# Attention outputs divided once per pair of heads, paired score banks, keys stacked by transfers, and TensorE held to program order

## The chip, the core and the metric

The kernel runs on one core of a Trainium2 chip. A core has TensorE (PE; its weight loads are shown as PEld), VectorE (DVE), ScalarE (ACT), GpSimd (POOL) and SyncE (SP, which here only issues transfers), and DMA queues that move data between its memories. Each engine works through its own instructions in their order and waits on semaphores for the others. The metric is the device time of one execution in microseconds (us).

## The reference

One layer of a diffusion backbone over 128 context tokens and 512 latent tokens with 1024 features. Two attention mixers are read in parallel from one input projection, merged, and followed by an MLP. What matters here, shortened:

```python
def _block_attention(q, k, v):                # mixer A: 8 query heads, 2 key heads
    s = einsum('bqgrd,bkgd->bgrqk', qblk, k) * scale
    p = softmax(s, axis=-1)
    return einsum('bgrqk,bkgd->bqgrd', p, v)

def _neighbourhood_attention(...):            # mixer B: 8 heads, a window of keys and a bias
    s_loc = where(col_mask, s_loc + bias, NEG_INF)
    p = softmax(concatenate([s_loc, s_ctx]), axis=-1)
    return p[..., :n_loc] @ v_window + p[..., n_loc:] @ ctx_v

a_o = _block_attention(aq, concat([ctx_ak, ak]), concat([ctx_av, av]))
b_o = _neighbourhood_attention(bq, bk, bv, ctx_bk, ctx_bv, nat_bias)
m = sigmoid(ga) * (a_o @ w_br_a) + sigmoid(gb) * (b_o @ w_br_b)
x = x + gate1 * (m @ w_out)
x = x + gate2 * (square(relu(h2 @ w_mlp_in)) @ w_mlp_out)
```

Latent queries of A read 128 context keys and 512 latent keys (640 columns); those of B read windows of 384 or 512 columns. Context queries read only context keys.

## The kernel before

Features lie on the 128 partitions, tokens (640 = 128 + 512) along the columns; a half is 320 columns. Each number is carried as a rounded upper part (`h`) and a rest (`l`), both float32r, and a product is three matmuls: upper x upper, upper x lower, lower x upper (`gemm_k`, L339 to L341). Each weight tile of 128 output features arrives by a transfer (`wst`), ACT makes its upper part (L301), POOL or DVE its lower part (L302). One tile of the input projection is 2 halves x 8 blocks x 3 = 48 matmuls of 320 columns.

**Stages.** A first stage makes norms and three tiles: A's keys, the first two query heads, A's values. Then comes attention (from about 59.5 us to 345 us), then the merge with the remaining gates, the output projection and the MLP.

**Attention.** `attention` walks through units: two heads (`HeadA`) and the context queries of that pair (`CtxPair`), four times, then the same for mixer B (`HeadB`). The score products `S` of a unit run beside the transposes `T` and value products (`pv`) of the unit before, step by step. For each block of 128 queries `S` multiplies into one or two PSUM banks (`pss`), DVE finds the maximum, ACT writes the exponentials (`pa`, `pb`) with their row sums, and `normalise` (L616) divides the weights on DVE: the row-sum's reciprocal (L618) and a product (L619). `T` transposes four blocks into a bank (`pt`, L653, L710), ACT and DVE split the result (`ph` L606, `pl` L607), and `pv`, called one step later, multiplies both with the values into `po`; `combine` adds the two halves of `po` into the output tile `ao` or `bo`, which holds two heads.

**Fill.** The other projection tiles (`AFILL`, `BFILL`: queries, keys, values, and four gates, which are stored to memory and read back in the merge, `GATES`) are cut into groups of three matmuls, and `F.spend` puts as many into each step as the constant `STEP` leaves. Work that follows a tile, such as norms, rotation and splits, is kept in `F.posts`.

**Order.** Outside the first stage a scheduler sets the order of each engine's instructions, TensorE's included. `manual_schedule` holds an engine to the order of the program; in the merge and MLP it is used for DVE.

**Keys.** A stacked key tile holds a head's keys twice, on partitions 0 to 63 and 64 to 127, since the queries' upper and lower parts lie on these halves. For A `k_both` (L568) writes both halves with ACT and DVE, in pieces; for B `k_part` writes one half and `k_dup` (L575) copies it by a transfer.

**PSUM.** One set of eight banks for the whole kernel: g 2 (fill), s 3 (scores), t 2 (transposes), o 1 (value products).

Of the kernel before, what the change touches and what calls it, by code (L numbers as in the profile page):

```python
# [42 lines left out]
Q0P = 2  # L43
# [14 lines left out]
def trunk_layer(ctx: ExitStack, tc: tile.TileContext, xT, small_in, wmodA, wmodB, tabs, cacheK, cacheV, bias,  # L58
# [10 lines left out]
    pp = ctx.enter_context(tc.tile_pool(name="pp", bufs=1, space=bass.MemoryType.PSUM))  # L69
# [27 lines left out]

    def ps_g():
        return pp.tile([P, 512], F32, tag="g", bufs=2, name="pg")

    def ps_s():
        return pp.tile([P, 512], F32, tag="s", bufs=3, name="pss")

    def ps_t():
        return pp.tile([P, 512], F32, tag="t", bufs=2, name="pt")

    def ps_o():
        return pp.tile([P, 512], F32, tag="o", bufs=1, name="po")
# [105 lines left out]
    class Weights:  # L214
# [74 lines left out]
        def conv(self):  # L289
# [4 lines left out]
            else:  # L294
# [7 lines left out]
                (nc.gpsimd if key in WPOOLSET else DVE).tensor_sub(lo, st, r32(hi))  # L302
# [207 lines left out]
    ck, cv = (kp.tile([P, NT], F32, name=x) for x in ("ck", "cv"))  # L510
    nc.sync.dma_start(ck, cacheK)
# [15 lines left out]
    def qk_norm(raw, g, h, bank=ps_g, src=None, buf=None):  # L527
        sl = HALVES[h]
        buf = buf or rf
        sq = buf("qsq")  # L530
        src = raw[:, sl] if src is None else src
        ACT.activation(sq[:, :HT], src, AF.Square)
        pt = bank()
        PE.matmul(pt[:, :HT], blk, sq[:, :HT], start=True, stop=True)
        rs = buf("qrs")
# [26 lines left out]
    def k_part(k, e, dst, src, eng=None):  # L562

        s = src[half(e)]
        ACT.activation(k[0][half(e), dst], s, AF.Copy)
        (eng or DVE).tensor_sub(k[1][half(e), dst], s, r32(k[0][half(e), dst]))

    def k_both(k, e, dst, src):  # L568

        k_part(k, e, dst, src)  # L570
        s = src[half(e)]
        ACT.activation(k[0][half(1 - e), dst], s, AF.Copy)
        DVE.tensor_sub(k[1][half(1 - e), dst], s, r32(k[0][half(e), dst]))

    def k_dup(k, e, n, q=MISC):  # L575
        for t in k:
            q.dma_start(r32(t[half(1 - e), :n]), r32(t[half(e), :n]))
# [5 lines left out]
    def v_stack(raw, cvp, bank=ps_g):  # L583
# [32 lines left out]
    def normalise(p, sm):  # L616
        rc = small("rc", 1)
        DVE.reciprocal(rc, sm)  # L618
        DVE.tensor_scalar(p, p, rc, None, op0=OP.mult)  # L619

    class HeadA:
# [3 lines left out]
        def __init__(self, hd):  # L625
            self.j, self.e, self.g = hd // 2, hd % 2, hd // 4
            self.need = ("aq", self.j)

        def S(self, qt):
# [4 lines left out]
            ps = [ps_s(), ps_s()]  # L634
            p = u("pa")
            n2, s2, nm, sm = small("n2"), small("s2"), small("nm", 1), small("sm", 1)
            for j in range(2):
                c = slice(P + j * HT, P + (j + 1) * HT)
                PE.matmul(ps[j][:, :HT], q, kh[:, c], start=True, stop=False)
                PE.matmul(ps[j][:, :HT], q, kl[:, c], start=False, stop=True)  # L640
                DVE.tensor_reduce(n2[:, j:j + 1], ps[j][:, :HT], axis=AX.X, op=OP.max, negate=True)
            DVE.tensor_tensor(nm, n2[:, 0:1], n2[:, 1:2], op=OP.min)  # L642
            for j in range(2):
                ACT.activation(p[:, HALVES[j]], ps[j][:, :HT], AF.Exp, bias=nm, accum_out=s2[:, j:j + 1])  # L644
            DVE.tensor_add(sm, s2[:, 0:1], s2[:, 1:2])
            normalise(p, sm)
            self.p.append(p)
            return 540

        def T(self, t):  # L650
# [5 lines left out]
            def pv():  # L656
# [7 lines left out]
                return 430  # L664
            return 250, pv
# [5 lines left out]
    class HeadB:  # L671
# [13 lines left out]
        def S(self, qt):  # L685
# [9 lines left out]
            mx, nm, sm = small("mx", 1), small("nm", 1), small("sm", 1)  # L695
# [3 lines left out]
            ACT.activation(p[:, :w], ps[:, :w], AF.Exp, bias=nm, accum_out=sm)  # L699
            normalise(p[:, :w], sm)  # L700
            self.p.append(p)
            return 380

        def T(self, gi):
# [9 lines left out]
            def pv():  # L714
# [11 lines left out]
                return 400  # L726
            return 230, pv

    class CtxPair:
# [28 lines left out]
        def T(self, _):  # L758
# [5 lines left out]
            def pv():  # L764
# [7 lines left out]
                return 430  # L772
            return 110, pv

    AQ, BQS, BK, BV = {}, {}, {}, {}
    AO = [None] * 4
# [11 lines left out]
    def fill_tile(n, F):  # L788
# [7 lines left out]
        for h in range(2):  # L796
# [3 lines left out]
            for k in range(KT):  # L800
                gemm_k(ps, w, H1, h, k, k, k == 0, k == KT - 1)
                yield 400
# [7 lines left out]
            else:  # L810
                if h == 0:
                    raw = o_tile("raw")
                ACT.activation(raw[:, sl], ps, AF.Copy)
            F.flush(1)
        F.flush()
        if kind == "aq":
            def last():
                qk_norm(raw, qg, 1)
                a_q_rot(j, raw)
            F.posts = [lambda: qk_norm(raw, qg, 0), last]  # L820
        elif kind == "bq":
            BQS[j] = qs
        elif kind == "bk":
            DQ[QO].dma_start(bkT[j], raw[:, 0:P])
            ckj = ck[:, (j + 1) * P:(j + 2) * P]
            BK[j] = []

            def k_post(e):
                k = (kt_tile("bkh"), kt_tile("bkl"))
                k_part(k, e, slice(P, 2 * P), ckj)  # L830
                k_part(k, e, slice(6 * P, 7 * P), ckj)
                k_part(k, e, slice(0, P), raw[:, 0:P])
                k_part(k, e, slice(2 * P, 6 * P), raw[:, P:NT])
                k_dup(k, e, 7 * P, DQ[QD])
                BK[j].append(k)
# [549 lines left out]
```

## Time and profile before

| | us |
|---|---|
| runs: median (lowest, highest) | 1001.46 (1000.43, 1001.6) |
| the profiled execution | 1000.66 |
| its span | 998.7 |
| PE busy in the span | 951.0 (95%) |
| DVE busy | 704.9 (71%) |
| ACT busy | 516.4 (52%) |
| POOL busy | 171.7 (17%) |

The page cuts the span into 40 slices of 25 us; each digit is the busy share in tenths, and PEclk the granted clock:

```profile
PE   7987899998899999999999999999999999999996
DVE  4468877788866788787677787678833884368644
PEclk8998999999999999999999999999999999999999
```

Matmuls are pipelined: one of 320 columns is in the pipe for about 310 ns, while the next starts after 147 ns. So a busy share of PE is above the share of its peak, and short waits show better in the weight loads.

### The profile page before, as it was taken

To read this page: it belongs to the slowest core of one execution; us is meant where nothing else is said; L and a number is where in the kernel's file an instruction comes from. 1 tells how busy PE (TensorE), PEld (TensorE's weight loads), DVE (VectorE), ACT (ScalarE), POOL (GpSimd) and SP (SyncE) were. 2 spreads that over 40 slices of the span, in tenths; PEclk is the share of its full clock that TensorE was granted. 3 is DMA by queue.
4 is the path that set the end of the run, shared out by engine and by line. 5 is a ranking of instruction groups with operands and counts; after the bars stand their busy time and mean duration, and the time that the engine had idled before them with its cause. 6 is when DMAs were issued, how large, how long until landed. Compare 5 with 4: busy or idle time off the path is not lost.

```text
span 998.7 us, 16550 instructions
## 1 busy us (share of the span) xinstructions
PE 951.0 (95%) x6317; PEld 906.1 (91%) x6317; DVE 704.9 (71%) x1577; ACT 516.4 (52%) x1117; POOL 171.7 (17%) x153
## 2 busy tenths in 40 slices
PE   7987899998899999999999999999999999999996
PEld 5776778887888999999999899999999999999996
DVE  4468877788866788787677787678833884368644
ACT  4475667666655664654333563237611663156542
POOL 0342232211322010200041200012200220012100
PEclk8998999999999999999999999999999999999999
DMA  9842101222443445654742243212221233120312
GB/s 348 207 169 73 32 28 40 69 49 77 122 102 94 133 154 189 215 155 163 238 135 80 69 148 107 86 63 84 90 84 40 85 101 90 64 71 37 107 42 106
DMA packets 34767, 108.47 MB, mean 109 GB/s; under 512 B 4320, under 2 KB 8032, under 8 KB 34688
## 3 DMA queue, kind: packets, MB, share of 16 engines
q1 hardware_dynamic: 27072, 82.63, 26.1%
q0 software_dynamic: 6464, 23.47, 7.9%
q10 hardware_dynamic: 1152, 1.31, 0.4%
q8 instruction: 49, 0.80, 0.3%
q14 instruction: 30, 0.25, 0.1%
HBM read 99.14 MB, written 4.60 MB: 104 GB/s over the span
## 4 chain that ended last, share of the span: by engine, by line
PE 64%; DVE 13%; ACT 8%; issue 4%; DMA 2%; POOL 1%; POOLq 0%; ACTq 0%; DVEq 0%; SPq 0%
PE pss L341 7%; PE pss L340 7%; PE pss L339 7%; PE pg L339 7%; PE pg L340 7%; PE pg L341 6%; PE pt L340 4%; PE pt L341 4%; PE pt L339 4%; DVE sr L260 3%; ACT wb L280 2%; DMA wst<-w 2%; PE pt L653 1%; ACT wh L301 1%; DVE pl L607 1%
## 5 line engine op out<-in xcount | busy, mean ns | idle before, releaser
L301 ACT ACTIVATE wh<-wst 128x1024 fp32r<-128x1024 f32 x84 | 88.7, 1056 | 112.6 <-PE pg L340 41.3
L302 DVE TENSOR_TENSOR wl<-wst,wh 128x1024 fp32r<-128x1024 f32 x53 | 64.8, 1223 | 63.1 <-ACT wh L301 63.0
L302 POOL TENSOR_TENSOR wl<-wst,wh 128x1024 fp32r<-128x1024 f32 x31 | 74.6, 2409 | 156.6 <-ACT wh L301 156.6
L992 DVE SCALAR_TENSOR_TENSOR mt<-wmt,cb 128x512 f32<-128x512 f32 x128 | 81.5, 687 | 0.0
L281 POOL TENSOR_TENSOR wb<-wst,wb 128x512 fp32r<-128x512 f32 x24 | 31.8, 1324 | 260.6 <-ACT wb L280 236.2
L341 PE MATMUL pss<-hidh,wl 128*128 128x320 f32 x216 | 67.0, 310 | 3.5 <-POOL wl L302 3.5
L339 PE MATMUL pss<-hidh,wh 128*128 128x320 f32 x216 | 66.7, 309 | 0.0
L340 PE MATMUL pss<-hidl,wh 128*128 128x320 f32 x216 | 66.7, 309 | 0.0
L607 DVE TENSOR_TENSOR pl<-pt,ph 128x512 fp32r<-128x512 f32 (+2 forms) x80 | 50.3, 633 | 19.0 <-ACT ph L606 18.0
L606 ACT ACTIVATE ph<-pt 128x512 fp32r<-128x512 f32 (+2 forms) x80 | 44.2, 554 | 31.3 <-PE pt L653 15.3
L280 ACT ACTIVATE wb<-sr 128x512 fp32r<-128x512 f32 x48 | 29.8, 627 | 51.5 <-DVE sr L260 37.6
L1161 DVE TENSOR_TENSOR hidl<-rl,hidh 128x320 fp32r<-128x320 f32 x64 | 37.5, 586 | 20.8 <-ACT hidh L1154 20.2
L988 POOL DMA_DIRECT2D wmt<-wmodB x32 | 17.1, 536 | 169.7 <-DVE mt L992 103.1
L281 DVE TENSOR_TENSOR wb<-sr,wb 128x512 fp32r<-128x512 f32 x48 | 36.0, 755 | 14.2 <-ACT wb L280 14.1
L339 PE MATMUL pg<-hidh,wh 128*128 128x320 f32 x144 | 44.5, 309 | 0.0
L340 PE MATMUL pg<-hidl,wh 128*128 128x320 f32 x144 | 44.5, 309 | 0.0
L341 PE MATMUL pg<-hidh,wl 128*128 128x320 f32 x144 | 44.5, 309 | 0.0
L341 PEld LDWEIGHTS pss<-hidh,wl 128*128 128x128 f32 x216 | 40.5, 188 | 4.2 <-POOL wl L302 4.2
L339 PE MATMUL pt<-hidh,wh 128*128 128x320 f32 x136 | 42.0, 309 | 0.0
L340 PE MATMUL pt<-hidl,wh 128*128 128x320 f32 x136 | 42.0, 309 | 0.0
L341 PE MATMUL pt<-hidh,wl 128*128 128x320 f32 x136 | 42.0, 309 | 0.0
L644 ACT ACTIVATE pa<-pss,nm 128x320 f32<-128x320 f32 x64 | 33.1, 523 | 16.0 <-DVE nm L642 15.8
(958 smaller groups left out, 3459.3 us busy)
## 6 DMA issues: line engine op xcount, KB each, us to landing
wst<-w SPq DMA_DIRECT2D x64, 512.0 KB, 3.6
wmt<-wmodB POOLq DMA_DIRECT2D x32, 512.0 KB, 3.9
wst<-w_in SPq DMA_DIRECT2D x31, 512.0 KB, 3.9
ms<-wmodA SPq DMA_DIRECT2D x16, 512.0 KB, 7.6
x<-xT SPq DMA_DIRECT2D x16, 320.0 KB, 5.9
bt<-bias SPq DMA_DIRECT2D x16, 320.0 KB, 3.8
wst<-w_br SPq DMA_DIRECT2D x8, 512.0 KB, 4.3
wst<-w_out SPq DMA_DIRECT2D x8, 512.0 KB, 3.5
```

The costliest lines, as they stand in the source:

```text
L280: ACT.activation(t[:, lo4], src, AF.Copy)
L281: later.append(lambda: (nc.gpsimd if name in BLKP else DVE).tensor_sub(t[:, hi4], src, r32(t[:, lo4])))
L301: ACT.activation(hi, st, AF.Copy)
L302: (nc.gpsimd if key in WPOOLSET else DVE).tensor_sub(lo, st, r32(hi))
L339: PE.matmul(ps, wh[:, k], xh[:, sl], start=first, stop=False)
L340: PE.matmul(ps, wh[:, k], xl[:, sl], start=False, stop=False)
L341: PE.matmul(ps, wl[:, k], xh[:, sl], start=False, stop=last)
L606: ACT.activation(ph[:, :n], pt[:, :n], AF.Copy)
L607: DVE.tensor_sub(pl[:, :n], pt[:, :n], r32(ph[:, :n]))
L644: ACT.activation(p[:, HALVES[j]], ps[j][:, :HT], AF.Exp, bias=nm, accum_out=s2[:, j:j + 1])
L992: DVE.scalar_tensor_tensor(t, st[:, q * 512:(q + 1) * 512], 1.0, r32(cb[2 * q + i][:, :512]), op0=OP.mult, op1=OP.mult, accum_out=parts[:, ...
L1161: DVE.tensor_sub(dst[1][:, sl], r[:, :HT], r32(dst[0][:, sl]))
```

## The change

1. **Division.** `normalise` is gone. ACT writes the row sums into one tile for each pair of heads (`row_sum`). `pair_sums`, called in the second `T` of the pair's second head, takes the reciprocal of that tile, spread to 128 x 512. `pair_norm` transposes it (four transposes) and multiplies the pair's output tile by it, after the pair's last `combine`. The context queries are divided as before.
2. **Banks.** PSUM is opened three times: g 2, s 3, t 2, o 1 ahead of the attention; for mixer A two double banks for scores (S), t 2, o 1, g 1; for mixer B and all that follows the first set again. One reduction and one exponential cover both banks of a step in A.
3. **Keys.** The context keys are brought by transfers next to the new ones (`kr`), ACT and DVE split the whole tile once (`k_split`), and `k_stack` makes the stacked tiles of both heads by six transfers: four out of the split tile, and two that overwrite one of its halves after these.
4. **Order on TensorE.** From the end of the first stage to the end of attention TensorE is held to the program's order. In a step: the scores, the fill, the transposes, the value products of the step before, and what is left to be divided. The step's constant is 2100 for A and 2500 for B, against 2050, and the costs charged against it are higher.
5. **Fill.** Gates 21 and 29 come first, 22 and 30 move, and 23 and 31 are new in the list: 21 tiles against 19, and the merge has 10 gate tiles against 12. More of the fill stands ahead of the first scores. POOL makes the lower part of these weight tiles in two pieces. The norm of queries and keys is cut into squares and scaling.

```diff
-AFILL = (1, 10, 2, 6, 3, 14, 21)
-BFILL = (11, 7, 15, 12, 8, 16, 13, 9, 17, 29, 22, 30)
-GATES = (21, 29, 22, 30)
-STEP = 2050
-EARLY = 4000
+AFILL = (21, 29, 1, 10, 2, 6, 3, 14, 22)
+BFILL = (30, 11, 7, 15, 12, 8, 16, 23, 13, 9, 17, 31)
+GATES = (21, 29, 22, 30, 23, 31)
+STEP = {"pa": 2100, "pp": 2500}
+UNIT = 440
...
+    BANKS = {"pp": {"g": 2, "s": 3, "t": 2, "o": 1}, "pa": {"S": 2, "t": 2, "o": 1, "g": 1}}
+    def ps_2():
+        return psum["p"].tile([P, 2, 512], F32, tag="S", bufs=2, name="pss")
...
+    def k_split(src, n):
+
+        t = kt_tile("kh"), kt_tile("kl")
+        ACT.activation(t[0][:, :n], src[:, :n], AF.Copy)
+        DVE.tensor_sub(t[1][:, :n], src[:, :n], r32(t[0][:, :n]))
+        return t
+
+    def k_stack(t, own, n, q):
+
+        o = kt_tile("kh"), kt_tile("kl")
+        for e in (1 - own, own):
+            for i in range(2):
+                for f in range(2):
+                    if e != own or f != own:
+                        q[i].dma_start(r32((t if e == own else o)[i][half(f), :n]), r32(t[i][half(e), :n]))
+        return (o, t) if own else (t, o)
...
-    def normalise(p, sm):
-        rc = small("rc", 1)
-        DVE.reciprocal(rc, sm)
-        DVE.tensor_scalar(p, p, rc, None, op0=OP.mult)
+    def pair_sums(mixer, j):
+        RC[mixer, j] = r_("rc")
+        DVE.reciprocal(RC[mixer, j].rearrange("p (q e d) -> p q e d", q=4, e=2),
+                       SUMS[mixer, j].rearrange("p (e q) -> p q e", e=2).unsqueeze(3).broadcast_to([P, 4, 2, 64]))
+
+    def pair_norm(mixer, j):
+
+        rc, o = RC[mixer, j], (AO if mixer == "a" else BO)[j]
+        rows = ps_t()
+        for qt in range(4):
+            PE.transpose(rows[:, qt * P:(qt + 1) * P], rc[:, qt * P:(qt + 1) * P], ident)
+        DVE.tensor_mul(o[:, P:NT], o[:, P:NT], rows)
...
             for j in range(2):
                 c = slice(P + j * HT, P + (j + 1) * HT)
-                PE.matmul(ps[j][:, :HT], q, kh[:, c], start=True, stop=False)
-                PE.matmul(ps[j][:, :HT], q, kl[:, c], start=False, stop=True)
-                DVE.tensor_reduce(n2[:, j:j + 1], ps[j][:, :HT], axis=AX.X, op=OP.max, negate=True)
-            DVE.tensor_tensor(nm, n2[:, 0:1], n2[:, 1:2], op=OP.min)
-            for j in range(2):
-                ACT.activation(p[:, HALVES[j]], ps[j][:, :HT], AF.Exp, bias=nm, accum_out=s2[:, j:j + 1])
-            DVE.tensor_add(sm, s2[:, 0:1], s2[:, 1:2])
-            normalise(p, sm)
+                PE.matmul(ps[:, j], q, kh[:, c], start=True, stop=False)
+                PE.matmul(ps[:, j], q, kl[:, c], start=False, stop=True)
+            DVE.tensor_reduce(nm, ps, axis=AX.XY, op=OP.max, negate=True)
+            ACT.activation(p.rearrange("p (a b) -> p a b", a=2), ps, AF.Exp, bias=nm, accum_out=row_sum("a", self.hd, qt))
...
+                    if self.e:
+                        after.append(lambda: pair_norm("a", self.j))
+                return 470
+            if t == 1 and self.e:
+                pair_sums("a", self.j)
+            return 520, pv
...
+    pe_order = ctx.enter_context(ExitStack())
+    pe_order.enter_context(tc.manual_schedule(engines={PE.engine}))
...
+    AK = k_stack(k_split(kraw, NT + P), 1, NT + P, (DQ[1],) * 2)
...
-                if prev is not None and i < prev.nT:
-                    c, new = prev.T(i)
-                    t += c
+                todo, after[:] = list(after), []
                 if cur_u is not None and i < cur_u.nS:
                     t += cur_u.S(i)
+                tail = prev is not None and i < prev.nT
+                F.spend(max(0, STEP[psum["kind"]] - t - (520 if tail else 0) - (470 if pend else 0) - 500 * len(todo)))
+                if tail:
+                    _, new = prev.T(i)
                 if pend is not None:
-                    t += pend()
+                    pend()
+                for f in todo:
+                    f()
                 pend = new
-                F.spend(max(0, STEP - t))
```

**TensorE, the third context pair of mixer A**, while the sixth head's weights are transposed. Before (L339 to L341 fill, L653 transposes, L660 and L661 value products with the upper and the lower part):

```order
L653 MATMUL pt<-pk,pa 128x128 x4
L339 MATMUL pg<-h4h,wh 128x320
L340 MATMUL pg<-h4l,wh 128x320
L341 MATMUL pg<-h4h,wl 128x320
L339 MATMUL pg<-h5h,wh 128x320
L660 MATMUL po<-ph,vst 128x512
L661 MATMUL po<-pl,vst 128x512
L340 MATMUL pg<-h5l,wh 128x320
L341 MATMUL pg<-h5h,wl 128x320
```

After (L360 to L362 fill, L694 transposes, L701 and L702 value products); the second transposes of that head stand in the first row, its third ones in the row before the last:

```order
L694 MATMUL pt<-pk,pa 128x128 x4
L701 MATMUL po<-ph,vst 128x512
L702 MATMUL po<-pl,vst 128x512
L360 MATMUL pg<-h5h,wh 128x320
L361 MATMUL pg<-h5l,wh 128x320
L362 MATMUL pg<-h5h,wl 128x320
L360 MATMUL pg<-h6h,wh 128x320
L361 MATMUL pg<-h6l,wh 128x320
L362 MATMUL pg<-h6h,wl 128x320
L694 MATMUL pt<-pk,pa 128x128 x4
L701 MATMUL po<-ph,vst 128x512
```

Before, the scheduler let value products into the middle of a fill group; after, they follow the next transposes in whole groups.

**VectorE, the same place.** Before, a sum (L645) and the division of the weights (L618, L619) stand between the lower parts `pl`:

```order
L607 TENSOR_TENSOR pl<-pt,ph 128x512
L645 TENSOR_TENSOR sm<-s_1296 128x1
L618 RECIPROCAL rc<-sm 128x1
L619 TENSOR_SCALAR pa<-pa,rc 128x640
L607 TENSOR_TENSOR pl<-pt,ph 128x512
```

After, the reciprocal for the pair (L655) stands between the second and the third `pl` of the head; L568 and L569 belong to the rotation of queries:

```order
L635 TENSOR_TENSOR pl<-pt,ph 128x512
L655 RECIPROCAL rc<-sm 128x512
L635 TENSOR_TENSOR pl<-pt,ph 128x512
L568 TENSOR_TENSOR rt<-raw,cos 128x512
L569 STREAM_SHUFFLE rot<-raw 128x512
L635 TENSOR_TENSOR pl<-pt,ph 128x512
```

The small operations have left, and one of 512 columns has come in ahead of the third `pl`.

**SyncE's queue at the start of attention**, after the change (`bt` is B's bias, `kh` and `kl` the stacked keys, `gate` the store of a gate, `wst` weight tiles):

```order
L252 DMA wst<-w_in 128x1024
L728 DMA bt<-bias 128x640 x4
L604 DMA kh<-kh 64x768 x2
L604 DMA kl<-kl 64x768 x2
L604 DMA kh<-kh 64x768
L898 DMA gate_639<-raw 128x640
L604 DMA kl<-kl 64x768
L252 DMA wst<-w_in 128x1024
```

The key transfers and the first gate's store are new between the bias and the sixth weight tile.

More of the change, by code (lines that the diff above doesn't have):

```diff
@@ L560, in qa_part, with kr_tile @@
         eng.tensor_sub(qs[half(1 - e)], raw[half(e)], r32(qs[half(e)]))
[L562 to L577, printed above, removed]
+    def kr_tile():
+        return kp.tile([P, 896], F32, tag="kr", bufs=1, name="kr")
+    def k_split(src, n):
[11 more added lines that the diff above has]
+        return (o, t) if own else (t, o)
     def v_cols(v, t0, n):
@@ L878, in spend @@
                 c = self.step()
+                if c == 0 and "S" in psum["n"]:
+                    return
                 if c is None:
@@ L883, in spend, with half_end @@
                 self.debt -= c
+        def half_end(self):
+            while self.cur is not None and self.step():
+                pass
         def until(self, what):
@@ L949, in attention @@
             pend()
+        while after:
+            after.pop(0)()
     todo = []
```

158 lines of the change are left out of this document (98 added, 60 removed).

## The prediction

> **What bounds the kernel now.** I read the busy time by stage first, then who TensorE waits for, then the groups of VectorE. Columns of the first: the stretch, its length, and the busy time (and count) of PE, its weight loads, DVE, ACT and POOL; then the granted clock, the DMA share and GB/s.
>
> ```profile
> span 998.7 us, 16550 instructions
> ...
> 59.50:79.50 20.00, 13.41 (x84) 11.98 (x82) 15.70 (x24) 14.45 (x34) 9.27 (x7) 0.94 0.62 213
> 79.50:220.40 140.90, 128.18 (x774) 111.44 (x775) 114.64 (x302) 93.86 (x254) 34.56 (x24) 0.98 0.16 45
> 220.40:345.00 124.60, 116.66 (x752) 106.04 (x752) 92.68 (x265) 76.63 (x192) 24.78 (x23) 1.00 0.36 98
> 345.00:540.00 195.00, 195.00 (x1326) 193.80 (x1325) 151.82 (x372) 92.00 (x178) 30.34 (x43) 1.00 0.54 175
> 79.50:90.00 10.50, 9.81 (x47) 8.56 (x47) 7.80 (x26) 5.90 (x18) 0.61 (x1) 0.79 0.01 2
> ```
>
> From 345 on PE never pauses: 195.0 us for 1326 matmuls, 147 ns each (nearly all have 320 columns). Nothing but less PE work helps there. Before that lies attention, in three stretches: getting the keys ready (59.5 to 79.5), mixer A (to 220.4), mixer B (to 345). PE idles 6.6, 12.7 and 7.9 us in them, 27.2 in all, and in 10.5 us it runs at clock 0.79. In mixer A DVE is busy 114.6 of 140.9 us, 81%. So attention is PE's work plus waits, and these rows say on whom. Of the matmuls:
>
> ```profile
> PE pss L639 <- DVE qs L560: 6.7, 1, 6.7
> PE pt L653 <- DVE pa L619: 4.8, 9, 1.1
> PE po L661 <- DVE pl L607: 3.5, 4, 1.6
> PE pss L639 <- ACT pa L644: 3.0, 4, 1.4
> PE po L768 <- DVE bo L614: 2.6, 2, 1.4
> PE pt L710 <- DVE nm L698: 1.6, 3, 1.0
> PE pt L653 <- DVE pl L607: 1.4, 1, 1.4
> PE po L722 <- DVE pl L607: 1.1, 2, 0.9
> ...
> PE pt L710 <- DVE pb L619: 0.4, 1, 0.4
> ```
>
> And of the weight loads, which stop before the matmuls that are still in the pipe:
>
> ```profile
> PEld pt L653 <- DVE pa L619: 7.7, 11, 1.3
> PEld pss L639 <- DVE qs L560: 6.9, 1, 6.9
> PEld po L661 <- DVE pl L607: 5.3, 7, 1.9
> PEld pss L639 <- ACT pa L644: 3.1, 7, 1.0
> PEld po L768 <- DVE bo L614: 3.1, 2, 1.7
> PEld pg L339 <- ACT raw L813: 2.9, 8, 0.8
> PEld pt L710 <- DVE nm L698: 2.4, 3, 1.2
> PEld pt L653 <- DVE pl L607: 2.1, 3, 1.6
> ...
> PEld po L722 <- DVE pl L607: 1.7, 3, 1.2
> ...
> PEld pt L710 <- DVE pb L619: 0.8, 2, 0.7
> ```
>
> Nearly all name DVE. The true loss of a wait lies between the two rows, since the pipe drains through a part of it; I take the middle.
>
> **The change, part by part.** Against the profiled execution's own time: 1000.66 us, 2.0 outside the span. The median of the runs shown, 1001.46, is 0.8 above it.
>
> *Start.* The chain of waits ahead of the first score product:
>
> ```profile
> 73.88 2.32 DVE akl L566
> ...
> 76.22 1.60 DVE akl L573
> ...
> 78.69 0.83 DVE qs L560
> 79.57 0.64 PE pss L639
> ```
>
> The keys' lower halves are eight DVE pieces there; after, one of 768 columns. And 120 matmuls of fill stand ahead of the first score instead of 72: 48 x 0.147 = 7.1 us, more than the 6.7 of the wait. In return the stacked copies must land. The nearest transfer (KB each, median us to landing):
>
> ```profile
> bkh<-bkh POOLq DMA_DIRECT2D x8, 224.0 KB, 5.8
> ```
>
> Without the pieces from 73.88 to 78.69 the keys and queries are split by 73.9; plus 5.8 is 79.7, and PE, which ran out of fill near 72.8 (79.57 less 6.7), comes at 79.9. The second head group's transfers go behind the first's, and no one needs them for two pairs of heads. On SP the gate's store and the sixth weight tile stand behind them; that tile is used some 25 us later. On POOL the last two key transfers of a B pair wait until the first four have landed, and the lower half of a weight tile is queued behind them; it is wanted a tile (48 x 0.147 = 7.1 us) or more later. Neither costs anything, nor does POOL's doing that half in two pieces. So -6.7, and +1.0 for a late landing (bounds 0 and 5.8). The slow clock followed on that idle time, 10.5 x 0.21 = 2.2 us; with it gone, -2.2.
>
> *Weights no longer divided, banks in pairs.* In mixer A (out<-in, count | busy, mean ns | idle before):
>
> ```profile
> L607 DVE TENSOR_TENSOR pl<-pt,ph 128x512 fp32r<-128x512 f32 x35 | 23.9, 684 | 7.7 <-ACT ph L606 7.6
> L619 DVE TENSOR_SCALAR pa<-pa,rc 128x640 f32<-128x640 f32 x31 | 18.1, 585 | 0.3
> L645 DVE TENSOR_TENSOR sm<-s 128x1 f32<-128x1 f32 x31 | 9.9, 320 | 2.9 <-ACT pa L644 2.9
> L642 DVE TENSOR_TENSOR nm<-n 128x1 f32<-128x1 f32 x32 | 7.1, 221 | 0.2
> L618 DVE RECIPROCAL rc<-sm 128x1 f32<-128x1 f32 x31 | 4.8, 156 | 0.3
> ...
> L606 ACT ACTIVATE ph<-pt 128x512 fp32r<-128x512 f32 x35 | 20.8, 597 | 15.0 <-PE pt L653 14.5 <-PE po L660 0.3
> ```
>
> L619, L645, L642 and L618 go: 39.9 us of DVE. The waits of the transposes on L619 go with them, 4.8 + 0.4 on PE, 7.7 + 0.8 on the loads: -7.0. Two double banks instead of three single ones end the score product's wait on the exponential: -3.0. The other waits on DVE (pl, nm, the combine bo) are 10.2 on PE and 14.6 on the loads, middle 12.4; DVE falls to some 60 to 65% of the stage, the reciprocals below included. I let three quarters go, -9.3 (bounds -4 and -14.6). The 32 reductions of two banks in place of 64 are part of that. ACT loses 32 exponential calls and stays below DVE.
>
> *Dividing the outputs.* Eight groups of four transposes are PE work that nothing hides:
>
> ```profile
> 62.60 0.66 PE L594 MATMUL pt<-pk,raw 128*128 128x128 f32 x4
> ```
>
> Four last 0.66 with the drain; 0.5 in a row with others. 8 x 0.5 = +4.0 (3 to 5.3). The eight products with the outputs are DVE work of 0.69 each off PE's path.
>
> The new **reciprocal of 128x512** is what I know least. Per pair it stands on DVE between the second and the third pl of the unit (the order rows of the change), and PE, now held to its written order, can do nothing past the product that reads the third. What the trace has of reciprocals:
>
> ```profile
> L443 DVE RECIPROCAL sc_e<-sc_e 128x16 f32<-128x16 f32 x1 | 0.3, 253 | 0.0
> ...
> L442 DVE TENSOR_SCALAR sc_e<-sc_e 128x16 f32<-128x16 f32 x1 | 0.2, 175 | 0.0
> ...
> L753 DVE RECIPROCAL cr<-cs 128x2 f32<-128x2 f32 x7 | 1.2, 165 | 0.2
> ```
>
> Sixteen elements cost 253 ns, where another operation takes 175 and two elements take 165: (253 - 165) / 14 = 6.3 ns for one more. So R = 0.165 + 510 x 0.0063 = 3.4 us. Bounds: 0.69, as the other operations of 512 columns, and 253 / 16 x 512 = 8.1. I take 3.4, the slope of the only rows there are.
>
> What covers it: in the third A pair, after the second transposes come the first two products (2 x 0.235, that is 147 ns x 512 / 320), six fill matmuls (0.88), transposes 0.5, products 0.47, three fill matmuls 0.44, transposes 0.5: 3.3 us until the product that needs the third pl. The chain beside it: ph 0.60, pl 0.68, R, pl 0.68, some 0.3 for handing over: 2.3 + R. PE waits R - 1.0. Counted so, the first B pair (seven groups of three fill matmuls between) waits R - 2.5; the other six lie between these. Together 8R - 15: at 3.4, +12.2 (bounds 0 and +50).
>
> The Trainium skill, "VectorE: DVE Perf Modes", in the part on the fixed hardware budget, says that a reciprocal runs as an iterative divide with a repeat count of 8. At the 0.96 GHz of its Specifications this would be 8.3 ns an element, by estimate 4.4 us for 512, and the sum 8 us higher than mine. The rows agree that it isn't one cycle (88 ns for 14 elements), not on the number.
>
> *Moved work.* Gates 23 and 31 leave the merge and come into attention: 2 x 48 matmuls, 14.1 us off one place and onto another, for nothing, since both are PE work at 147 ns. Their stores and loads join those of four others. With one fill bank in mixer A each half tile waits for its copy; the row of L813 has 0.36 us a time with two banks. +1.0 more (0 to 5).
>
> **Sum.** -6.7 + 1.0 - 2.2 - 7.0 - 3.0 - 9.3 = -27.2; +4.0 + 12.2 + 1.0 = +17.2. Net -10.0: 990.7 us.
>
> **Rivals.** *DVE's relief goes further.* All waits of the loads quoted go (36.0 with the 0.8) and the clock's 2.2, against 6.0 of new costs and the reciprocal: 1000.66 - 38.2 + 6.0 = 968.5 with it hidden, 980.7 with it at 12.2; middle 975. For it speaks that DVE was at 81%; against it, that the same engine gets a long instruction at eight places.
>
> *A steeper slope.* If the floor of 165 hides part of the slope and the fixed part is 0.12, one element costs (253 - 120) / 16 = 8.3 ns, R = 4.4, the term is 20.2: 998.7. It fits the rows as well as mine does. It is also what the Trainium skill's "VectorE: DVE Perf Modes" would make of it.
>
> *Slower: the reciprocal holds PE.* The gain without it is 27.2 - 5.0 = 22.2, so the sign turns at R = (22.2 + 15) / 8 = 4.65, and over 0.2% slower from 4.9 (9.3 ns an element). At the upper bound 8.1 the time is 1000.66 - 22.2 + 49.8 = 1028. Against it: it needs a fixed part under 105 ns, while the operation beside it takes 175 in all.
>
> **How the numbers follow.** Forecast (982 to 997) 0.40; further relief 0.28; steeper slope 0.18; slower 0.14. A measurement tells some 0.2% (2 us) from no change. Of the third case 0.08 is faster, 0.07 the same, 0.03 slower: faster 0.76, same 0.07, slower 0.17. The range runs from 969, which leaves out the lower third of the relief, to 1004, which leaves out most of the slower case.
>
> **What would show it.** The duration of the 128x512 reciprocal, first: 3.4 or longer. PE's idle time ended by pl in the units of the context heads: eight waits of 1 to 3 us behind a reciprocal. No wait ahead of the first score, and clock 1.00 from 80 to 90. No wait of a transpose on the exponential's output, none of a score on ACT. The merge unchanged at 147 ns. I am wrong if PE in its written order waits elsewhere, at products one step behind their transposes or at the single fill bank, for more than 5 us; or if the reciprocal's waits don't appear though it is long.

## The result, and the profile after

The change makes the kernel slower: 1017.44 us (median of 4 runs, 1016.87 to 1017.68) against 1000.94 for the kernel before beside it (4 runs, 999.79 to 1001.6). The ratio is 1.0169, with an interval of 1.0153 to 1.0185. The forecast was 990.7, so it missed the sign and, with its own range of 969 to 1004, the time. One execution further below (E11) ran in a slower state, 1180.69 us at a mean granted clock of 0.746, and no time or ratio here counts it.

The profiled execution took 1017.35 us, its span is 1015.3. First the busy time by stage, with the columns of the table that the prediction shows (the stretch, its length, busy time and count of PE, its loads, DVE, ACT, POOL; clock, DMA share, GB/s). The stages now begin at other times: keys from 58.4, mixer A from 78.4, B from 230.9, merge and output projection from 383.3, and the first weights of the MLP from 561.9:

```profile
58.40:78.40 20.00, 20.00 (x133) 19.35 (x132) 12.36 (x20) 12.12 (x26) 13.06 (x13) 1.00 0.86 271
78.40:230.90 152.50, 127.92 (x792) 116.16 (x790) 95.27 (x139) 87.21 (x191) 35.25 (x33) 0.96 0.16 47
230.90:383.30 152.40, 141.26 (x929) 132.01 (x927) 90.51 (x202) 79.96 (x190) 37.06 (x48) 1.00 0.42 114
383.30:561.90 178.60, 175.16 (x1186) 173.69 (x1186) 145.95 (x349) 87.44 (x173) 33.04 (x44) 1.00 0.53 171
561.90:627.20 65.30, 61.02 (x390) 59.55 (x389) 49.65 (x108) 34.62 (x71) 10.63 (x9) 0.95 0.38 118
78.40:89.00 10.60, 9.04 (x62) 8.77 (x61) 3.30 (x4) 5.97 (x13) 2.82 (x3) 1.00 0.35 105
```

Three promises of the change are kept. PE is busy for all of the first 20 us, where it idled 6.6 before. The clock right after is 1.00 where it was 0.79. And DVE fell from 81% to 62% of mixer A (95.27 of 152.50 us). Yet mixer A got longer, 152.5 us for 792 matmuls where it took 140.9 for 774. A helper that is less busy has not made the engine that waits for it faster.

The waits of PE over the whole execution (of the matmuls: us in total, times, longest) name what it meets now:

```profile
PE po L701 <- DVE ao L642: 5.7, 3, 4.1
PE po L816 <- DVE ao L642: 4.8, 3, 2.1
PE pg L360 <- DVE qs L579: 4.7, 2, 4.3
PE pt L360 <- ACT hh6h L386: 4.2, 1, 4.2
...
PE po L816 <- DVE bo L642: 3.1, 5, 1.1
PE po L766 <- DVE pl L635: 2.8, 4, 1.7
PE po L702 <- DVE pl L635: 2.7, 4, 1.9
PE pss L684 <- POOL qs L585: 2.6, 1, 2.6
```

Two kinds of wait that the change meant to remove are gone: none of a transpose on divided weights, none of a score on the exponential. In their place stand waits for the one output bank (`po` behind the combine of `ao` and `bo`) and for the one fill bank of mixer A (`pg` behind `qs`). The waits behind `pl`, which were to shrink too, stayed: 5.7 us in attention where they were 6.0. Over the whole of attention all waits of the matmuls add up to 35.2 us in 33 pieces; before they were 26.7 in 31.

Now the groups that the prediction priced (mixers A and B; count | busy, mean ns | idle before):

```profile
L635 DVE TENSOR_TENSOR pl<-pt,ph 128x512 fp32r<-128x512 f32 x56 | 38.4, 686 | 25.9 <-ACT ph L634 25.2
L655 DVE RECIPROCAL rc<-sm 128x512 f32<-128x512 f32 x8 | 26.8, 3344 | 0.1
```

The reciprocal, the least known price, was right: 3.34 us against 3.4.

What one such wait looks like shows the timeline of mixer A (start us, length us, operation). PE first:

```profile
103.79 0.60 PE L694 MATMUL pt<-pk,pa 128*128 128x128 f32 x4
108.45 0.79 PE L701 MATMUL po<-ph,vst 128*128 128x512 f32 x1 [4.06 <-DVE ao L642]
```

and DVE in the same time:

```profile
104.08 0.69 DVE L571 TENSOR_TENSOR raw<-rt,rot 128x512 f32<-128x512 f32 x1
...
104.98 2.22 DVE L803 TENSOR_SCALAR pc<-pc,cr 128x128 f32<-128x128 f32 x2
107.12 0.68 DVE L635 TENSOR_TENSOR pl<-pt,ph 128x512 fp32r<-128x512 f32 x1
107.72 0.67 DVE L642 TENSOR_TENSOR ao<-po,ct 64x512 f32<-64x512 f32 x1
```

PE's next instruction writes the output bank, which the combine at 107.72 must empty first, and that stands behind a rotation and the context heads' division. PE has other work, but its order lets it reach none of it. A second place, where the long reciprocal stands ahead of what empties the fill bank (this wait is not one of the order alone: it is there in the free order of E1 too):

```profile
146.32 0.39 PE L702 MATMUL po<-pl,vst 128*128 128x512 f32 x1
150.99 0.60 PE L360 MATMUL pg<-h0h,wh 128*128 128x320 f32 x1 [4.29 <-DVE qs L579]
...
145.71 3.33 DVE L655 RECIPROCAL rc<-sm 128x512 f32<-128x512 f32 x1
149.08 0.48 DVE L579 SCALAR_TENSOR_TENSOR qs<-pg,qs 64x320 fp32r<-64x320 f32 x1
...
150.35 0.49 DVE L579 SCALAR_TENSOR_TENSOR qs<-pg,qs 64x320 fp32r<-64x320 f32 x1
```

The last new wait is late, where the output projection hands over to the MLP (the chain that ended last; start, length):

```profile
565.13 4.65 DVE mt L1072 x8
569.90 0.16 DVE parts L1057
...
570.37 2.70 DVE parts L1055
573.09 1.27 DVE xm L381 x4
574.36 0.60 DVE hh6l L389 x2
```

`mt` are pieces of the late modulation, 128 products on DVE that run beside the merge. The last ones that the norm ahead of the MLP needs now start at 565 to 569 us, and the norm waits for them; in the kernel before they started by 534, well ahead of the MLP's first product at 550.

**Where the time went, by stage.** For each stage the table gives its length less the PE work in it: every matmul counted at the distance at which its kind follows another when nothing waits (147 ns for 320 columns, 231 for 512, 109 for a transpose). What is left is loss, in us of one profiled execution:

| loss | before | change | free order (E1) | best (E7) |
|---|---|---|---|---|
| keys | 7.3 | 0.0 | 0.1 | 0.0 |
| mixer A | 26.6 | 36.3 | 22.9 | 18.4 |
| mixer B | 16.0 | 18.3 | 6.0 | 7.2 |
| merge and output projection | 0.2 | 4.7 | 3.0 | 0.8 |
| first weights of the MLP | 2.8 | 7.9 | 7.9 | 3.1 |
| sum | 52.9 | 67.2 | 39.9 | 29.5 |

Losses rose by 14.3, work by 3.6 (the 32 transposes, and some); the ends of the span gave back 1.3. That is the 16.6 us between the spans. The stage ahead of the table's varies from 55.8 to 59.3 us between kernels whose work there is the same, so single differences of 2 or 3 us in one profile say little.

**Part of the loss is a slower clock.** The half-speed stretch of the kernel before (6.83 us from 77.15) did not vanish but moved: the change has three in mixer A and one at the first weights of the MLP, each beginning in a wait of PE of 2.6 us or more or right behind it (the third of mixer A, not shown, runs from 195.24 to 198.66):

```profile
106.50:113.32 6.82, 4.87 (x17) 4.68 (x18) 6.62 (x6) 2.56 (x4) 4.74 (x5) 0.50 0.57 144
150.87:154.28 3.41, 3.29 (x12) 3.32 (x13) 1.98 (x3) 1.33 (x2) 0.48 (x1) 0.50 0.36 125
...
574.12:580.95 6.83, 6.58 (x19) 5.45 (x20) 2.84 (x8) 2.19 (x6) 0.00 (x0) 0.50 0.22 72
```

In these stretches a matmul of 320 columns follows the last after 0.27 us instead of 0.147. An estimate from that and from PE's busy time in them (11.6 us in the three of mixer A, 6.6 in the MLP, 4.4 in the stretch before): the slower clock costs some 5 us in mixer A and 3 in the MLP, where it cost 2 before. So some 6 of the 14.3 us are clock, in the wake of waits. No run here separates waits and clock.

### The profile page after: what moved, and what is told of

Its sections match the earlier page's. It is cut to its first block, busy times and chain, and to the rows that moved or that the text cites. A ratio compares the mean times of both kernels' runs of the same rounds, so it can differ in the third digit from the quotient of the medians.

```text
span 1015.3 us, 16376 instructions
## 1 busy us (share of the span) xinstructions
PE 952.2 (94%) x6349; PEld 914.2 (90%) x6349; DVE 673.9 (66%) x1333; ACT 500.0 (49%) x1026; POOL 190.6 (19%) x196
## 5 line engine op out<-in xcount | busy, mean ns | idle before, releaser
L321 POOL TENSOR_TENSOR wl<-wst,wh 128x512 fp32r<-128x512 f32 (+1 forms) x54 | 83.9, 1570 | 179.7 <-ACT wh L318 171.0
L323 DVE TENSOR_TENSOR wl<-wst,wh 128x1024 fp32r<-128x1024 f32 x51 | 62.3, 1221 | 61.0 <-ACT wh L318 61.0
L362 PE MATMUL pss<-hidh,wl 128*128 128x320 f32 x208 | 64.4, 309 | 1.1 <-POOL wl L321 1.1
L360 PE MATMUL pss<-hidh,wh 128*128 128x320 f32 x208 | 64.3, 309 | 0.0
L361 PE MATMUL pss<-hidl,wh 128*128 128x320 f32 x208 | 64.3, 309 | 0.0
L362 PE MATMUL pg<-hidh,wl 128*128 128x320 f32 x144 | 44.6, 310 | 1.1 <-POOL wl L321 1.1
L362 PE MATMUL pt<-hidh,wl 128*128 128x320 f32 x144 | 44.6, 310 | 1.0 <-POOL wl L321 1.0
L360 PE MATMUL pt<-hidh,wh 128*128 128x320 f32 x144 | 44.5, 309 | 0.0
L360 PE MATMUL pg<-hidh,wh 128*128 128x320 f32 x144 | 44.5, 309 | 0.0
L361 PE MATMUL pt<-hidl,wh 128*128 128x320 f32 x144 | 44.5, 309 | 0.0
L686 DVE TENSOR_REDUCE nm<-pss 128x1 f32<-128x640 f32 x32 | 26.3, 821 | 24.4 <-PE pss L685 24.1
L362 PEld LDWEIGHTS pss<-hidh,wl 128*128 128x128 f32 x208 | 39.0, 188 | 1.3 <-POOL wl L321 1.3
```

What stands on the lines that cost most here:

```text
L321: nc.gpsimd.tensor_sub(lo[:, ks], st[:, ks], r32(hi[:, ks]))
L323: DVE.tensor_sub(lo, st, r32(hi))
L360: PE.matmul(ps, wh[:, k], xh[:, sl], start=first, stop=False)
L361: PE.matmul(ps, wh[:, k], xl[:, sl], start=False, stop=False)
L362: PE.matmul(ps, wl[:, k], xh[:, sl], start=False, stop=last)
```

## The experiments

The theory after the result: **the order written out for TensorE costs the time**, since PE stops at the first instruction that is not ready, wherever it is. The rivals: the long reciprocal; the banks; the moved gates; DVE's order, which a scheduler still chooses. All ratios are to the kernel before on the same chip; differences in us are between medians, and where two runs come from different chips the ratios give slightly other numbers. Every edit is made on the changed kernel, except in E12.

**E1, no written order on TensorE.**

```diff
-    pe_order.enter_context(tc.manual_schedule(engines={PE.engine}))
```

> The changed kernel with one line less: TensorE is not held to program order in attention, the scheduler orders it as before. If the written order is what makes TensorE stand still (its waits on the single output bank and the single fill bank, 26 us of waits over 0.3 us), the time falls by 8 to 15 us, to 1002 to 1009. If the waits come from VectorE's long reciprocal whatever the order, it stays within 3 us of 1017.4.

989.73 us, ratio 0.9899 (0.9884 to 0.9914): 27.7 us below the change (27.0 by the ratios), more than the 8 to 15 expected. The waits of PE in attention fall from 35.2 us to 12.6 in 14 pieces. Of those for the output bank one is left:

```profile
PE pg L360 <- DVE qs L579: 4.0, 1, 4.0
PE po L701 <- DVE ao L642: 1.9, 1, 1.9
```

This line alone turns the change from slower to faster. The clock is not what does it, since mixer A's mean granted clock is 0.96 in both:

```profile
76.60:215.70 139.10, 126.70 (x791) 114.58 (x790) 95.73 (x139) 86.89 (x190) 35.71 (x33) 0.96 0.18 53
```

The wait of 4.0 us is the one shown above at 150.99, behind the long reciprocal; the free order keeps it.

**E2, the reciprocal of the eight sums instead of 512 columns.**

```diff
-        DVE.reciprocal(RC[mixer, j].rearrange("p (q e d) -> p q e d", q=4, e=2),
-                       SUMS[mixer, j].rearrange("p (e q) -> p q e", e=2).unsqueeze(3).broadcast_to([P, 4, 2, 64]))
+        DVE.reciprocal(SUMS[mixer, j], SUMS[mixer, j])
+        DVE.tensor_copy(RC[mixer, j].rearrange("p (q e d) -> p q e d", q=4, e=2),
+                        SUMS[mixer, j].rearrange("p (e q) -> p q e", e=2).unsqueeze(3).broadcast_to([P, 4, 2, 64]))
```

> The reciprocal is taken of the eight sums, and a copy spreads it to 128x512, in place of a reciprocal of 512 columns. VectorE is held some 0.9 us at each of the eight places instead of 3.34. If that instruction is what TensorE waits behind, the time falls by 8 x (1 to 2) = 8 to 16 us, to 1001 to 1009. If the waits on the output and fill banks are their own, it falls by less than 5 us.

1008.12 us, ratio 1.0077 (1.0048 to 1.0106), 9.3 below the change and still slower than before. The two groups that take the place of 26.8 us are

```profile
L656 DVE COPY rc<-sm 128x512 f32<-128x512 f32 x8 | 7.2, 894 | 0.0
L655 DVE RECIPROCAL sm<-sm 128x8 f32<-128x8 f32 x8 | 1.6, 202 | 2.8 <-ACT pa L688 1.4 <-ACT pb L745 1.1
```

18.0 us less on DVE bring half as much. The long reciprocal is a part of the loss, not its main part.

**E3, late modulation at a faster pace.**

```diff
-MCOST = 1600
+MCOST = 1400
```

> One constant: the modulation work on VectorE in the merge is paced at 1400 instead of 1600, so that the 20 calls that are left with ten gate tiles issue about as many steps as 24 did. If the 7 us that TensorE loses near 560 to 570 us come from steps that are pressed into the second norm, the time falls by 5 to 7 us, to 1010 to 1012, and attention is unchanged. If they come from something else, nothing changes.

1021.25 us, ratio 1.0213 (1.0197 to 1.0228). A miss: the MLP's loss falls from 7.9 to 3.1 as it should, but merge and output projection lose 12.6 instead of 4.7. The DVE work is the same in sum and meets PE elsewhere.

**E4, the three edits together.**

> The three edits together (scheduler's order, reciprocal of the eight sums, pace 1400). If they are separate causes the gains add: 1017.4 less the sum of the three. If the free order and the short reciprocal take away the same waits, it is less than the sum by 5 us or more.

990.83 us, ratio 0.9904 (0.9883 to 0.9925), no better than E1 alone; the single gains and the loss of E3 would add up to 984.2. Attention loses 25.3 us instead of E1's 29.0, but merge, output projection and MLP lose 15.4 instead of 10.9. What the short reciprocal gains, the late stages take back. The faster pace lost time there in E3 too; E7 has the old pace and the gates back, so what each of the two does to this isn't separated.

**E5, gates 23 and 31 back in the merge**, with the written order.

```diff
-BFILL = (30, 11, 7, 15, 12, 8, 16, 23, 13, 9, 17, 31)
-GATES = (21, 29, 22, 30, 23, 31)
+BFILL = (30, 11, 7, 15, 12, 8, 16, 13, 9, 17)
+GATES = (21, 29, 22, 30)
```

> The changed kernel with gates 23 and 31 back in the merge (four gates in the fill instead of six). TensorE's work is the same in sum. If the merge, the output projection and the first MLP tiles are held by VectorE's modulation work as soon as 14 us of TensorE's work leave them (12.6 us lost there against 3.0 before the change), the loss goes back to about 3 and the time falls by 8 to 10 us, to 1007 to 1009. If moving gates is free, as the prediction had it, the time stays within 2 us of 1017.4.

1019.41 us, ratio 1.0187 (1.0168 to 1.0206): a miss, no gain that the intervals can tell. The late part of the theory holds: output projection and MLP lose 3.2 us instead of 9.4. But mixer B now loses 26.8 instead of 18.3. With 14.1 us of work less it gets only 5.6 us shorter:

```profile
230.60:377.40 146.80, 129.04 (x833) 119.52 (x832) 90.14 (x202) 76.44 (x184) 31.86 (x44) 0.99 0.40 107
```

So under the fixed order the fill that is taken out mostly leaves holes.

**E6, a second output bank and a second fill bank in mixer A**, paid for with one of the two double score banks, so that the set stays at eight.

```diff
-    BANKS = {"pp": {"g": 2, "s": 3, "t": 2, "o": 1}, "pa": {"S": 2, "t": 2, "o": 1, "g": 1}}
+    BANKS = {"pp": {"g": 2, "s": 3, "t": 2, "o": 1}, "pa": {"S": 1, "t": 2, "o": 2, "g": 2}}
```

> The changed kernel with other banks in mixer A: one double bank for scores, two for fill, two for outputs, in place of 2, 1 and 1. If TensorE in its written order stands still because the one fill bank or the one output bank is not yet read, A's loss of 36 us falls by 8 to 14 us and the time to 1003 to 1009. If the engines behind are late in any case, the waits move to the transposes and scores, and with one score bank the time stays or rises by up to 10 us.

1035.07 us, ratio 1.0349 (1.0332 to 1.0366), 17.6 above the change and beyond the 10 of its second case. The waits of A's products on `ao` are gone and `pg` on `qs` is down to 0.4, but

```profile
PE pss L684 <- ACT pa L687: 20.4, 20, 1.9
PE po L702 <- DVE pl L635: 9.5, 11, 3.1
```

So the waits for the output bank and the fill bank are real, but within a set of eight banks they were exchanged, and this exchange is a bad one: a score product then waits for the exponential before it.

**E7, the best of it:** no written order (E1), the short reciprocal (E2), the two gates back (E5), and the late pace as it was.

> Scheduler's order, the reciprocal of the eight sums, and the two gates back in the merge, pace as in the change. If order, reciprocal and gates are separate causes: 989.7, less some 4 for the reciprocal (as A's loss fell from 22.9 to 18.5 with all three edits), less 8 for the merge: 976 to 979. If the merge's loss comes from elsewhere: 984 to 988.

978.26 us, ratio 0.9776 (0.9757 to 0.9794): 2.2% below the kernel before, as expected, and 39 us below the change. PE in the three stretches A, B, and merge with output projection:

```profile
76.10:210.70 134.60, 125.63 (x792) 114.00 (x791) 86.49 (x143) 86.73 (x190) 36.75 (x33) 0.97 0.19 55
210.70:335.70 125.00, 122.62 (x818) 115.01 (x817) 82.28 (x207) 75.06 (x183) 32.39 (x44) 1.00 0.45 126
342.00:526.70 184.70, 184.45 (x1254) 183.80 (x1254) 148.89 (x374) 85.79 (x165) 30.22 (x39) 1.00 0.51 170
```

Against E9 (below) only the reciprocal differs: the ratios are 0.0088 apart, some 9 us, as much as in the written order (E2).

**E8, each row divided as before, free order.** The pair's reciprocal and its transposes go, 64 divisions of weights come back:

```diff
+    def normalise(p, sm):
+        rc = small("rc", 1)
+        DVE.reciprocal(rc, sm)
+        DVE.tensor_scalar(p, p, rc, None, op0=OP.mult)
...
-                    if self.e:
-                        after.append(lambda: pair_norm("a", self.j))
...
-            if t == 1 and self.e:
-                pair_sums("a", self.j)
```

(and the same in B.)

> Scheduler's order on TensorE as in e1_free_order, and each row of weights divided again as before the change (no reciprocal of 512 columns, no transposes for it). If dividing once per pair relieves VectorE, as the prediction had it, the time rises from 989.7 by 5 to 15 us. If the long reciprocal and the transposes eat the relief, it stays within 4 us of 989.7.

991.96 us, ratio 0.9918 (0.9903 to 0.9933), beside E1's 0.9899: the intervals overlap. Dividing once per pair, as the change does it, is worth some 2 us, if anything. It frees DVE of the divisions, but puts the long reciprocals on it and 32 transposes on TensorE.

**E9, gates back, free order.** E1 with the edit of E5.

> The change without the written order on TensorE, and gates 23 and 31 back in the merge; the long reciprocals stay. Beside the run without the written order alone (989.73 us) and the one that also has the short reciprocals (978.26). Theory: the two gates in attention push the late modulation steps past the merge; with them back norm2 and the first weight tiles lose some 6 us less, while attention, free to reorder, gives up the 14.1 us of gate work in full: 982 to 985, so that the short reciprocals are worth the remaining 4 to 7. Rival: the gates fill gaps of attention that stay empty without them, as in the written order (where putting them back gained nothing): 988 to 991, and the whole 11 us belong to the reciprocal.

987.76 us, ratio 0.9864 (0.9835 to 0.9892). Between the two forecasts and nearer the rival's: some 3 us below E1, with intervals that overlap. Output projection and MLP lose 3.2 us instead of E1's 9.5; the merge and B lose 3.7 more.

**E10, each row divided (E8), with the written order.**

> The change with its written order, but each row of weights divided as before: no 128x512 reciprocals, no 32 transposes, 64 normalisations instead (32 of about 0.59 us in mixer A, 32 of 0.4 in B, with a reciprocal of 0.16 each). Theory: the written order costs because TensorE stops at each late piece of VectorE, whichever it is; VectorE gets busier by some 15 us while the eight long blocks go: 1008 to 1025, within 10 of the change. Rival: nearly all of the loss is the long reciprocal and the transposes behind it: 1000 to 1006.

1015.62 us, ratio 1.0140 (1.0108 to 1.0171). With no long reciprocal in the kernel the written order still costs 23.7 us (E8 to E10; 22.2 by the ratios), and the same places wait:

```profile
PE po L708 <- DVE ao L642: 5.8, 3, 3.6
PE po L817 <- DVE ao L642: 4.9, 2, 3.5
PE pg L360 <- ACT raw L874: 4.8, 5, 1.6
```

So the way of dividing is not what makes the written order cost so much. Without the long block, ordinary pieces of DVE and ACT stand ahead of the same banks.

**E11, DVE held to the written order as well.**

```diff
-    pe_order.enter_context(tc.manual_schedule(engines={PE.engine}))
+    pe_order.enter_context(tc.manual_schedule(engines={PE.engine, DVE.engine}))
```

> The change with VectorE held to the written order as well as TensorE. Theory A: TensorE stops because the scheduler, which still chooses VectorE's order, puts rope, q parts and reciprocals ahead of the combines and products that TensorE's fixed order needs next; with both in one order these waits go and the time falls to 990 to 1008. Theory B: any fixed order loses, since a late piece then holds everything behind it on that engine too, VectorE waiting for ScalarE's copies and exponentials: 1020 to 1060.

1021.85 us (median of three), ratio 1.0217 (1.0188 to 1.0247). This lies at the lower edge of theory B's range, and theory A falls. The waits on the combines shrink and those on `pl` grow:

```profile
PE pg L360 <- DVE qs L579: 5.9, 3, 3.6
PE po L702 <- DVE pl L635: 5.7, 4, 3.3
...
PE po L701 <- DVE ao L642: 4.2, 3, 2.2
```

The wait of 4.06 us at 108.45 is 2.23 here, so the scheduler's order for DVE has a share in single waits, but holding DVE too doesn't lower the sum.

**E12, the kernel before with a written order on TensorE**, from the same place to the end of attention.

```diff
+    pe_order = ctx.enter_context(ExitStack())
+    pe_order.enter_context(tc.manual_schedule(engines={PE.engine}))
...
+    pe_order.close()
```

> The kernel before, with TensorE held to the order of its code from the end of the first projections to the end of attention, as the change does it; nothing else. Its code was not laid out for it (transposes of a step ahead of the scores, fill at the end of each step). Theory: the written order costs by itself, whatever the rest: 1015 to 1060. Rival: the loss belongs to the change's single banks and long reciprocals, and before loses less than 5 us: 1000 to 1005.

1060.62 us, ratio 1.0597 (1.0563 to 1.0632). The rival (the loss belongs to the change's banks and reciprocals) falls; the loss is just above the theory's range. The scores, value products of B and transposes that waited 3.0, 2.6 and 4.8 us before wait now

```profile
PE pss L639 <- ACT pa L644: 18.4, 16, 2.8
PE po L768 <- DVE bo L614: 9.3, 4, 3.5
PE pt L653 <- DVE pa L619: 8.0, 4, 3.8
```

All waits in attention are 68.7 us against 26.7, and the mean granted clock there is 0.92 against 0.99, so the 59 us hold slow clock too. Some 10 of them fall ahead of attention: the first fill product starts at 69.0 us instead of 59.0, behind products for norms and transposes that stand first in this code. The written order costs 27.7 us in the change and 59 here, so the change suits it better, by its layout, its banks or its costs; which of these it is, no run shows. None of them pays for the order.

## Why the prediction was wrong

**The step that failed** is the pricing of the written order. The prediction saw that PE is "now held to its written order" and applied it to one wait, that for the third `pl` behind a reciprocal. For all other waits it kept the change's relief, "I let three quarters go, -9.3", and for the fill bank "+1.0 more (0 to 5)". The output bank got no term. The waits behind `pl`, `nm` and the combine `bo`, priced at three quarters gone, are 10.2 us on PE before, 10.9 in the change and 2.0 in the free order (E1). The runs show the order to cost 27.7 us in the change (E1), some 22 to 24 without the pair division (E10 against E8) and 59 in the kernel before (E12). The prediction named this at its end, as what would make it wrong "for more than 5 us", but gave it neither a price nor a chance; the rival on the slow side hung on the reciprocal alone.

The trace of before gave a warning that the prediction read as a gain. Of its 26.7 us of waits in attention, 11.8 remain without those of the keys (6.7), of the divided weights (4.8 and 0.4) and of the score banks (3.0). They stood there although the scheduler could place fill in them. A written order has to do at least as well at each of these places by hand. No row of that trace prices it when it doesn't; E12 does, for that code.

In numbers, by the losses of the table: in keys and mixers A and B the terms of the sum (without the transposes, which are work) give -14.0, measured +4.7, a miss of 18.7. In the late stages the sum has nothing, measured +9.6. Work and the ends of the span came out 1.7 below. Together 26.6, which is the distance from 990.7 to 1017.35.

Point by point:

- **Start**: right. The wait of 6.7 us is gone and PE was busy throughout; the late landing (+1.0) did not show.
- **Clock** (-2.2): right at its place, 1.00 after the start where 0.79 stood; wrong in the sum, since half-speed stretches came back behind the new waits and cost some 5 us in mixer A.
- **Divided weights and score banks** (-7.0, -3.0): right. Both kinds of wait are gone in the profile after.
- **Other waits on DVE** (-9.3): wrong in the change, as above. Without the written order the relief is there: attention as a whole loses 29.0 us in E1 against 49.9 before, 20.9 less, more than the 14.0 of the sum.
- **Transposes** (+4.0): right in size; the work rose by 3.6.
- **Reciprocal**: its length was right (3.34 against 3.4); its price was mis-sized, 12.2 against the 9.3 that E2 recovers (8.8 without the written order), with a broadcast copy of 0.89 us left in its place. The way it was to be paid came true in part: instead of eight waits of 1 to 3 us behind `pl` there are five, 4.7 us in all, and two of them above 1 us. In the third A pair, worked out at 2.4, it is 1.89. The longest wait behind a reciprocal, 4.29, is at the fill bank, where no term put it.
- **Fill bank** (+1.0, 0 to 5): too small. In mixer A the matmuls wait 9.0 us for it, 4.3 of them behind a reciprocal, as just said.
- **Moved gates** ("for nothing"): wrong. They take 14.1 us of PE work out of the stretch in which DVE does its 128 modulation products, and the last ones that the norm needs come late. Output projection and MLP lose 6.2 us less with the gates back (E5, E9). What that is worth to the whole differs: nothing that can be told in the written order, some 2 to 3 us in the free one.
- **The rivals**: the steeper slope falls with the 3.34 us, and so does the slow case as it was told, which began at 4.65. The relief did go further (E1), but only where PE isn't held. The time ended on the slow side through a mechanism that had no rival of its own.
- **The merge "unchanged at 147 ns"**: nearly; with the output projection it lost 4.7 us against 0.2.

That E1 ran at 989.73, a microsecond from the forecast, is no proof of the sum: its attention gained more than forecast and its late stages lost 7.9 us that the sum didn't have.

**What stays open.** Why the written order meets more waits at one place than at another was not taken apart further; E6 and E11 show only that neither a different share of the banks nor an order for DVE removes them. How much of the cost is waiting and how much the slower clock behind the waits isn't separated. How much of E1's gain each single wait holds isn't known, since removing one moves the next up.

## What to carry to other kernels

- Before an engine is fixed to program order, add up the waits that it has *with* a scheduler's freedom. In the kernel before these grew from 26.7 to 68.7 us under a fixed order; in the change places at the one output bank and the one fill bank joined. Whether a second bank or a step more of distance at each of them would save the order was not shown: E6, which could only exchange banks, lost.
- Less work on a helper engine helps only where the piece that is waited for arrives earlier. DVE lost 19 points of its share in mixer A and PE waited more.
- Work taken out of a full stretch of PE uncovers what ran beside it. Look for the other engine's work in that stretch (here 128 products of 0.69 us) before calling a move free; and take a reciprocal on the few numbers, then spread it.

## What the hardware showed that was not expected

**A reciprocal is paid by the element.** 128x512 took 3344 ns, 128x8 202 ns, 128x2 166 ns: (3344 - 202) / 504 = 6.2 ns an element, and a product of the same 512 columns takes 0.69 us. The Trainium skill, "VectorE: DVE Perf Modes", in the part on the fixed hardware budget, speaks of a repeat count of 8. The slope here is 6.0 cycles at the 0.96 GHz of its Specifications, and the runs decide.

**A short operation of DVE can take the time of one on POOL.** The addition `parts` L1055 of four elements, in the late chain above, took 2.70 us; one like it just before, L1057, 0.16. POOL in that time (start, length):

```profile
570.67 2.35 POOL L321 TENSOR_TENSOR w<-wst,w 128x1024 fp32r<-128x1024 f32 x1
```

POOL's operation ends at 573.02, the addition at 573.07, though by the records it began 0.30 us earlier than POOL's. The two context divisions at 104.98, ahead of the first wait shown, took 2.22 us together, where the median of one is 0.29. They stretched in the same way beside

```profile
104.14 2.98 POOL L321 TENSOR_TENSOR wl<-wst,wh 128x512 fp32r<-128x512 f32 x2 [12.58 <-ACT wh L318]
```

Part of that wait of PE may so come from POOL, through DVE. The Trainium skill, "SBUF — State Buffer", in the part on who interferes with whom, has DVE and GpSimd share a pair of ports that one of them holds for a whole instruction. The ends here agree with it; the recorded start of the addition, ahead of POOL's, does not, so this stays a reading. No run here took the POOL work away, so its share of the loss wasn't measured.
